# A two-layer diffusion backbone: the first FFN's input half by seven products of quarters, layer 1's adaLN rows beside its output half and the gMLP, the gMLP in a written order

## The chip, the cores and the metric

The kernel runs on one core of a Trainium2 chip. A core has five engines with instruction streams of their own: TensorE (PE: matrix products; PEld is its weight load), VectorE (DVE), ScalarE (ACT), GpSimd (POOL) and SyncE (SP), whose queue issues all the DMAs here. The metric is the device time of one execution, in microseconds (us); less is better.

## The reference, cut to what matters

Two layers over 512 tokens of width 1024. Each layer modulates its input by six rows (shift, scale and gate, for the mixer and for the FFN) made from a conditioning vector, mixes tokens (layer 0: windowed attention; layer 1: a gated MLP over chunks, the gMLP), and then runs a SwiGLU FFN of hidden size 2816.

```
mod_l = silu_c @ ada_w[i] + ada_b[i]
sh_ml, sc_ml, g_ml, sh_fl, sc_fl, g_fl = [m[:, None, :] for m in jnp.split(mod_l, 6, axis=-1)]
h_l = modulate(rmsnorm(x, norm_g[i, 0]), sh_ml, sc_ml)
...                                     # the token mixer gives y_l
x = x + g_ml * rmsnorm(y_l, norm_g[i, 1])
f_l = swiglu(modulate(rmsnorm(x, norm_g[i, 2]), sh_fl, sc_fl), ffn_w_in[i], ffn_w_out[i])
x = x + g_fl * rmsnorm(f_l, norm_g[i, 3])

def swiglu(h, w_in, w_out):
    gate, up = jnp.split(h @ w_in, 2, axis=-1)
    return (jax.nn.silu(gate) * up) @ w_out
```

## The kernel before

All products keep float32 precision by splitting each operand into a high part rounded to the matmul's type (`high`, L197, on ScalarE) and the rest (`low`, L200, mostly on VectorE), and adding three matmuls: high x high, high x low, low x high.

Tokens are four tiles of 128 (t). Weights stream in units of 128 x 2048 (1 MB) through `ws` (two raw buffers, tag raw; four buffers each for the high and low halves). An FFN's input half has 22 units, one for each block of 128 hidden columns (gate and up). Units 0 and 1 are done token tile by token tile (`head`: tiles fa, fat) while the tokens of the turn before still come in. Units 2 to 21 are done by `rest`. The output half is `down`: 11 units, each two blocks of 128 rows; for each unit and token tile 12 matmuls of 512 columns into tile y. Its last two units form the turn: as each token tile's y is done, a `Chain` squares it (ScalarE), makes the root (GpSimd), applies the gate row and adds the residual (`gain_y`, `add_x`, VectorE), squares again, multiplies by the scale row (`gain_x`, GpSimd, L1126), adds the shift row (`shift_x`, VectorE, L1130), and TensorE transposes the result (`turn`, tile hT, L1137), which is split into H, the next stage's input. In the turn out of the attention, tiles 2 and 3 first `merge` a part that was made earlier (L1098).

Layer 0's `rest` makes 8 x 3 matmuls of 512 columns for gate and as many for up: 48 a unit (L1328 to L1330). Layer 1's FFN uses `seven`: the product of the 2 x 2 quarters of H with the 2 x 2 quarters of the unit's weights by seven products with sums and differences of quarters (Strassen's scheme in Winograd's form). Each product is 4 x 3 matmuls of 256 columns, 84 a unit (L1456). The sums of H are made once (`prepare`, inside the turn before: `rebuild` L1375 adds H's parts back on GpSimd, `sum_a` adds on VectorE, and the sums are split); the four differences of each unit's weights by GpSimd (`diff`, L1420); three chains of products collect in PSUM and are combined by `keep`, `up1`, `up2` (L1467), `gate1`, `silu` and `gates`.

The adaLN rows of `Ada(layer, s)`: eight chunks of weights are scaled and added up on VectorE (`add`, L340, tile acc from ada_raw), the sum is split, summed over partitions by two matmuls a half with ones (`total`, L364, tile ada_ps), and `done` (L370 to L374) makes the row. Rows (0, 5) and (1, 0) to (1, 3) are made as a background generator in layer 0's `rest`, four steps a unit; (1, 4) in `down` and the gMLP; (1, 5) in layer 1's `seven`. Their transfers share the tag raw with the weights.

What sets the order: a step is put at a time by `at`, or by its rank in the list ORDER if it stands there; `run_plan` emits the steps, and inside `tc.manual_schedule()` the engines keep that order. Outside of it a scheduler orders the instructions. Before, the turns and layer 1's input half are in a written order; layer 0's `rest`, the output halves' first units and the gMLP are the scheduler's. Each engine runs its own stream in order; the SP queue too.

Of the kernel before, what the change touches and what calls it, by code (L numbers as in the profile page):

```python
# [14 lines left out]
P = 128  # L15
D = 1024
# [134 lines left out]
c0turned_hi_1 wfetch_12 c0turned_hi_0 c1shift_x_1 whigh_12_0 c0turned_lo_0 wlow_11_1 c1turn_0 c0turned_lo_1 c3merge
c1turn_1 head_0_0 c1turned_hi_1 c1turned_hi_0 c2add_x c3gain_y c1turned_lo_1 c1turned_lo_0 head_0_1 c2square_x
c2gain_x c2rstd_x c3square_y c3rstd_y head_1_0 c2shift_x_0 c2shift_x_1 c3add_x c2turn_0 head_0_2 c2turn_1
c2turned_hi_0 c3gain_x c3square_x c3rstd_x c2turned_hi_1 head_1_1 c2turned_lo_0 c2turned_lo_1 whigh_12_1 head_2_0
c3shift_x_0 c3shift_x_1 head_1_2 c3turn_0 c3turn_1 c3turned_hi_1 c3turned_hi_0 c3turned_lo_0 wlow_12_0 c3turned_lo_1
head_2_1 wlow_12_1 head_3_0 head_2_2 head_3_1 head_3_2 work_9_0 wfetch_44 work_10_0 whigh_43_0 whigh_43_1
c0square_y#2 work_9_1 wlow_43_1 work_10_1 work_9_2 wlow_43_0 whigh_44_0 c0rstd_y#2 c0gain_y#2 c0add_x#2 c0gain_x#2
c0square_x#2 c0rstd_x#2 c0shift_x_0#2 c0turn_0#2 work_10_2 whigh_44_1 c1square_y#2 c0shift_x_1#2 wfetch_45
c1rstd_y#2 c1gain_y#2 c1add_x#2 c0turn_1#2 <lambda>_1_2 c1square_x#2 <lambda>_2_2 wlow_44_1 c2square_y#2 c1gain_x#2
whigh_45_0 c1rstd_x#2 work_9_3 c2rstd_y#2 c2gain_y#2 c1shift_x_1#2 c1shift_x_0#2 work_10_3 c2add_x#2 c1turn_0#2  # L160
c0turned_hi_0#2 c0turned_hi_1#2 c2gain_x#2 c0turned_lo_0#2 c1turn_1#2 c3square_y#2 <lambda>_3_2 c1turned_hi_0#2
c1turned_hi_1#2 <lambda>_0_2 c0turned_lo_1#2 c1turned_lo_0#2 <lambda>_0_0 c2square_x#2 c1turned_lo_1#2 c2rstd_x#2
c2shift_x_0#2 <lambda>_1_0 c2shift_x_1#2 wlow_44_0 c3rstd_y#2 c2turn_0#2 c2turn_1#2 c2turned_hi_1#2 c2turned_hi_0#2
c3gain_y#2 c3add_x#2 <lambda>_0_1 c3square_x#2 c2turned_lo_0#2 c3gain_x#2 c3rstd_x#2 <lambda>_2_0 c3shift_x_0#2
c3shift_x_1#2 c2turned_lo_1#2 <lambda>_1_1 c3turn_0#2 whigh_45_1 c3turn_1#2 wlow_45_1 c3turned_hi_0#2
c3turned_hi_1#2 <lambda>_2_1 c3turned_lo_0#2 <lambda>_3_0 c3turned_lo_1#2 wlow_45_0 <lambda>_3_1 wfetch_56
whigh_55_0 work_2_0#2 wlow_55_0 work_3_0#2 whigh_55_1 c0square_y#3 wlow_55_1 whigh_56_0 c0rstd_y#3 c0gain_y#3
# [12 lines left out]
""".split()  # L180


@with_exitstack
def backbone_kernel(ctx: ExitStack, tc: tile.TileContext, a, out):
    nc = tc.nc

    def pool(name, **kw):
        return tc.tile_pool(name=name, bufs=1, reuse_waits="tile", **kw)

    base = ctx.enter_context(pool("base"))  # L190

# [185 lines left out]
    def ada(layer, sections, bank):  # L377
# [18 lines left out]
        for _ in range(4):  # L396
            yield
# [1402 lines left out]
```

## Time and profile before

| | us |
|---|---|
| median of 3 runs (lowest 1154.72, highest 1157.93) | 1154.83 |
| the profiled execution, its own time | 1155.57 |
| its span, first to last instruction | 1153.8 |
| busy: PE 1135.3, DVE 771.0, ACT 507.6, POOL 359.3 | |

The profile is of one execution. Its busy times are sums over each engine's instructions; times in rows are us from the span's start unless marked ns. `x1030` counts instructions, and `<-` names what released a wait. A matmul's own duration overlaps its neighbours', so its cost is read from the spacing of starts. The granted TensorE clock is 0.999 of full speed over the span.

### The profile page before, as it was taken

What the parts mean: (1) busy time and instruction counts of PE and PEld (TensorE: products, weight loads), DVE (VectorE), ACT (ScalarE), POOL (GpSimd) and SP (SyncE); (2) the same over time, 40 slices, a digit from 0 to 9 for tenths busy, and PEclk for the clock granted to TensorE, in tenths of its full rate; (3) what the DMA queues carried; (4) which work ended last, traced back from release to release, by engine and by line L of the source; (5) the groups of instructions that cost most, each with busy time, mean ns of one, the idle gap of its engine ahead of it and who ended that gap; (6) DMA issues with size and microseconds to landing.
All of it is one profiled execution on the core that took longest, in us unless ns stands there. A gap on an engine that the chain in (4) does not pass through costs nothing.

```text
span 1153.8 us, 16530 instructions
## 1 busy us (share of the span) xinstructions
PE 1135.3 (98%) x6638; PEld 974.6 (84%) x6638; DVE 771.0 (67%) x1030; ACT 507.6 (44%) x853; POOL 359.3 (31%) x265
## 2 busy tenths in 40 slices
PE   8999999999999999999999999999999999999997
PEld 5789887778988888888888788889999999998886
DVE  6778989857555566653445758448989998953325
ACT  6357778654313221242233535335454555443322
POOL 2357475514100000000000413007778788700000
PEclk9999999999999999999999999999999999999999
DMA  9633222242155576642435241322133343324221
GB/s 367 273 135 128 78 107 74 97 157 93 74 207 172 204 255 219 223 146 106 167 125 182 87 169 73 110 74 73 56 139 138 126 147 128 129 73 145 74 73 74
DMA packets 25297, 158.10 MB, mean 137 GB/s; under 512 B 3322, under 2 KB 3578, under 8 KB 8452
## 3 DMA queue, kind: packets, MB, share of 16 engines
q1 hardware_dynamic: 25220, 157.04, 38.1%
q8 instruction: 52, 0.85, 0.3%
q14 instruction: 25, 0.20, 0.1%
HBM read 154.94 MB, written 2.10 MB: 136 GB/s over the span
## 4 chain that ended last, share of the span: by engine, by line
PE 84%; DVE 7%; POOL 2%; DMA 2%; issue 2%; ACT 2%; SPq 0%; DVEq 0%; POOLq 0%; ACTq 0%
PE y L252 25%; PE f L1456 13%; PE f L1328 6%; PE f L1330 6%; PE f L1329 6%; PE v L252 3%; PE o_ps L929 2%; PE pT_ps L909 2%; PE s_ps L875 1%; PE u L1690 1%; PE u L1692 1%; PE u L1691 1%; DVE w_lo L200 1%; POOL T L1420 1%; PE s_ps L876 1%
## 5 line engine op out<-in xcount | busy, mean ns | idle before, releaser
L200 DVE TENSOR_TENSOR w_lo<-w_raw,w_hi 128x1024 fp32r<-128x1024 f32 x129 | 171.4, 1336 | 182.9 <-ACT w_hi L197 181.4
L197 ACT CAST w_hi<-w_raw 128x1024 fp32r<-128x1024 f32 x142 | 147.8, 1051 | 308.6 <-PE y L252 140.1
L252 PE MATMUL y<-w_hi,st 128*128 128x512 f32 x928 | 251.1, 390 | 0.0
L252 PEld LDWEIGHTS y<-w_hi,st 128*128 128x128 f32 x928 | 173.6, 188 | 36.0 <-DVE st L200 0.3
L252 PE MATMUL y<-w_lo,st 128*128 128x512 f32 x464 | 144.1, 389 | 0.0
L340 DVE SCALAR_TENSOR_TENSOR acc<-ada_raw,sc,acc 128x1024 f32<-128x1024 f32 x72 | 94.2, 1308 | 61.0 <-DMA ada_raw<-in_ada 60.0
L1328 PE MATMUL f<-H,w_hi 128*128 128x512 f32 x320 | 124.8, 390 | 0.0
L1330 PE MATMUL f<-H,w_lo 128*128 128x512 f32 x320 | 124.6, 389 | 0.0
L1329 PE MATMUL f<-H,w_hi 128*128 128x512 f32 x320 | 124.5, 389 | 0.0
L225 POOL TENSOR_TENSOR ry<-ry,mhalf 128x1 f32<-128x1 f32 x16 | 9.2, 577 | 368.1 <-DVE ry L222 228.6
L252 PEld LDWEIGHTS y<-w_lo,st 128*128 128x128 f32 x464 | 87.1, 188 | 18.3
L1456 PE MATMUL f<-H,w_hi 128*128 128x256 f32 x480 | 89.4, 284 | 1.2 <-DVE fc L1467 1.2
L1420 POOL TENSOR_TENSOR T<-w_raw 128x512 f32<-128x512 f32 x40 | 75.6, 1911 | 36.2 <-DMA w_raw<-in_w 27.0
L1456 PEld LDWEIGHTS f<-H,w_hi 128*128 128x128 f32 x480 | 74.9, 192 | 1.9 <-DVE fc L1467 1.6
L200 DVE TENSOR_TENSOR w_lo<-T,w_hi 128x1024 fp32r<-128x1024 f32 x40 | 72.4, 1809 | 3.4 <-ACT w_hi L197 3.3
L331 POOL MEMSET acc<- 128x1024 f32 x10 | 9.5, 956 | 200.9 <-DVE acc_st L200 200.8
L1330 PEld LDWEIGHTS f<-H,w_lo 128*128 128x128 f32 x320 | 60.1, 188 | 12.6
L1329 PEld LDWEIGHTS f<-H,w_hi 128*128 128x128 f32 x320 | 60.1, 188 | 12.5
L1328 PEld LDWEIGHTS f<-H,w_hi 128*128 128x128 f32 x320 | 60.1, 188 | 12.4
L903 POOL TENSOR_SCALAR p<-p,st 128x512 f32<-128x512 f32 (+1 forms) x64 | 55.9, 889 | 43.6 <-DVE st L899 21.6
L1456 PE MATMUL f<-H,w_lo 128*128 128x256 f32 x240 | 68.0, 283 | 1.0 <-DVE w_lo L200 1.0
L1456 PE MATMUL f<-S,w_hi 128*128 128x256 f32 x320 | 59.3, 283 | 0.0
(246 smaller groups left out, 2514.0 us busy)
## 6 DMA issues: line engine op xcount, KB each, us to landing
w_raw<-in_w SPq DMA_DIRECT2D x87, 1024.0 KB, 4.9
ada_raw<-in_ada SPq DMA_DIRECT2D x36, 1024.0 KB, 4.9
ada<-in_ada SPq DMA_DIRECT2D x8, 1024.0 KB, 10.1
ada_k<-in_ada SPq DMA_DIRECT2D x8, 512.0 KB, 5.7
row<-in_norm_g SPq DMA_DIRECT2D x7, 512.0 KB, 6.7
xin<-in_x SPq DMA_DIRECT2D x4, 512.0 KB, 5.4
x<-in_x SPq DMA_DIRECT2D x4, 512.0 KB, 3.7
out<-x SPq DMA_DIRECT2D x3, 512.0 KB, 2.6
```

What stands on the lines that cost most here:

```text
L197: nc.scalar.copy(out=hi, in_=src)
L200: (eng or nc.vector).tensor_tensor(out=lo, in0=src, in1=hi.bitcast(F32), op=ALU.subtract)
L252: nc.tensor.matmul(dst, l, w[:, n * 512:(n + 1) * 512], start=first and i == 0, stop=last and i == 2)
L340: nc.vector.scalar_tensor_tensor(out=ac, in0=w, scalar=sc[:, k:k + 1], in1=ac, op0=ALU.mult, op1=ALU.add)
L903: nc.gpsimd.tensor_scalar(out=p, in0=p, scalar1=self.st[:, 12 + j:13 + j], scalar2=1.0, op0=ALU.mult, op1=ALU.mult)
L909: nc.tensor.transpose(ps[:, j * P:(j + 1) * P], self.probs[j][:, i * P:(i + 1) * P], ident)
L929: nc.tensor.matmul(self.o[z * HD:(z + 1) * HD, c], v, pt[:, c], start=i < 2, stop=i >= self.nb - 2, tile_position=(0, z * HD), skip_group_ ...
L1328: nc.tensor.matmul(dst, hi, H[:, k, :], start=k == 0, stop=False)
L1329: nc.tensor.matmul(dst, hi, H[:, KC + k, :], start=False, stop=False)
L1330: nc.tensor.matmul(dst, lo, H[:, k, :], start=False, stop=k == KC - 1)
L1420: nc.gpsimd.tensor_tensor(out=T[i], in0=x, in1=y, op=op)
L1456: nc.tensor.matmul(dst, l[:, w], r[:, k, :], start=first and k == 0 and j == 0, stop=k == 3 and j == 2, skip_group_check=True)
```

## The change

1. Layer 0's FFN uses the seven products too: `rest` is now what `seven` was, for both layers, and `first=f0.prepare` puts the sums of its H into the turn out of the attention. Layer 0 keeps the PSUM tiles of two banks (`slot`); its chains 0 and 1 use the two banks of one tile. The written order goes on from that turn to the first steps of the output half.
2. The first half of the sums' sources (`first_half` in place of `rebuild`) is copied from PSUM by ScalarE, in both layers.
3. Row (0, 5) is made in layer 0's `rest` as (1, 5) in layer 1's, by chunks. Rows (1, 0) to (1, 3) are summed beside layer 0's output half (39 steps over its nine first units) from transfers into the two buffers of tag big; (1, 0) and (1, 1) are split whole (`spread`) and finished inside the turn into the gMLP (`rows_b`); (1, 2), (1, 3) and all of (1, 4) in the gMLP.
4. The gMLP's steps, before in program order under the scheduler, are put at times by `at`; ORDER has new ranks for the three turns and for the gMLP (none of its lines is shown).

```diff
-        def rebuild(self, q, t):
+        def first_half(self, q, c):
             name = ("S1", "S4")[q]
-            if t == 0:
+            if c.t == 0:
                 self.sums[name] = self.sum_tile(stage32)
-            dst = self.sums[name][:, :, t * P:(t + 1) * P]
-            hi, lo = (v[:, :, t * P:(t + 1) * P].bitcast(F32) for v in self.A["12" if q else "11"])
-            nc.gpsimd.tensor_tensor(out=dst, in0=hi, in1=lo, op=ALU.add)
+            nc.scalar.copy(out=self.sums[name][:, :, c.t * P:(c.t + 1) * P],
+                           in_=c.pt[:, q * 512:(q + 1) * 512].rearrange("p (k s) -> p k s", k=4))
...
+        def chain(self, n, ch):
+            if ch == 1 and self.bank is slot:
+                return self.pair[n][:, 512:768]
+            self.pair[n] = ps = self.bank(f"f{ch}")
+            return ps[:, 0:256]
...
-        def seven(self):
+        def one_banked(self):
             psM.__exit__(None, None, None)
...
+        def rest(self, nxt_of, head, **kw):
-            T, last, u0 = 10.08, NFF - 1, self.u0
+            T, last, u0, f2 = 10.08, NFF - 1, self.u0, F2[self.layer]
...
-            m5 = Ada(1, 5)
+            m5 = Ada(self.layer, 5)
...
-            run(bg)
+            run(bg, -(-left // (nu - 2 - v)))
+            left -= -(-left // (nu - 2 - v))
...
+    def sums(e, of):
+        e.start(nc.gpsimd)
+        yield
+        for k in range(KC):
+            if k % 2 == 0:
+                e.fetch(k // 2, of)
+            e.add(k)
+            yield
+    def rows_a():
+        for e in m1[:4]:
+            yield from sums(e, big)
+            if e.s < 2:
+                e.fetch_gain()
+                e.spread(f0.p)
+                yield
+    def rows_b(ch):
+        for i, (s, c) in enumerate(((1, 0), (1, 512), (0, 0), (0, 512))):
+            at(7 + .1 * i, m1[s].total, c, slot)
+            at(7.5 + .1 * i, m1[s].done, c)
...
-    f0.rest(to_gmlp, lambda t, n: n < 2 and v_part(t, (n,)), bg)
+    f0.rest(to_gmlp, lambda t, n: n < 2 and v_part(t, (n,)), lend=f0.lend, bg=rows_a(), bg_steps=39, also=rows_b)
...
+    U = 21.8
+    for u in range(4):
+        b = U + 10.9 * u + (2.6 if u == 3 else 0)
         for z in range(2):
+            at(b + 5.45 * z, u_part, u, z)
+            at(b + 5.45 * (z + 1) + .2, gelu_u, u, z)
+            at(b + 5 + 2.5 * z, ws.high, GU + u + 1, z)
+            at(b + 6 + 2.5 * z, ws.low, GU + u + 1, z, nc.vector)
+        at(b - 2, ws.fetch, GU + u + 1)
...
+    for i, e in enumerate(m1[2:4]):
+        at(-6, e.fetch_gain)
+        for c in (0, 512):
+            at(6 + 4 * i + c / 256, e.halve, c, nc.vector)
+            at(25 + 2 * i + c / 512, e.total, c, slot)
+            at(25.6 + 2 * i + c / 512, e.done, c)
...
+    with tc.manual_schedule():
+        run_plan()
```

In the rows of the order that follow, each row is one instruction, or several alike; L200 and L340 of before are L220 and L360 in the changed kernel, L252 is L272, L364 and L365 are L390 and L391.

VectorE in the input half of layer 0's FFN, one unit of before (act is the gated block):

```order
L340 SCALAR_TENSOR_TENSOR acc<-ada_raw,sc,acc 128x1024 x2
L200 TENSOR_TENSOR w_lo<-w_raw,w_hi 128x1024
L340 SCALAR_TENSOR_TENSOR acc<-ada_raw,sc,acc 128x1024 x2
L200 TENSOR_TENSOR w_lo<-w_raw,w_hi 128x1024
L1315 TENSOR_TENSOR act<-f,silu 128x512
```

and one unit of the changed kernel (T holds the differences of weight quarters, fc and f the chains):

```order
L220 TENSOR_TENSOR w_lo<-T,w_hi 128x1024
L220 TENSOR_TENSOR x_4082<-w_raw,x_4082 128x512
L1459 TENSOR_TENSOR act<-fc,silu 128x512
L220 TENSOR_TENSOR w_lo<-T,w_hi 128x1024
L1451 TENSOR_TENSOR f_4122<-f_4122,fc 128x256
L220 TENSOR_TENSOR w_lo<-w_raw,w_hi 128x1024
L1447 TENSOR_TENSOR fc<-f_4050,fc 128x256
L1443 TENSOR_TENSOR fc<-f_4050,fc 128x256
L368 SCALAR_TENSOR_TENSOR acc<-ada_k,sc,acc 128x1024
```

The sums over ada_raw have left the unit; four splits, the combining of the chains and, in every second unit, one chunk of row (0, 5) have come.

VectorE in the output half of layer 0's FFN, about one unit of before (st is the split of a block of act):

```order
L340 SCALAR_TENSOR_TENSOR acc<-ada_raw,sc,acc 128x1024 x2
L200 TENSOR_TENSOR w_lo<-w_raw,w_hi 128x1024
L200 TENSOR_TENSOR st<-act,st 128x512
L200 TENSOR_TENSOR w_lo<-w_raw,w_hi 128x1024
L200 TENSOR_TENSOR st<-act,st 128x512
```

and at the same place of the changed kernel:

```order
L220 TENSOR_TENSOR st<-act,st 128x512
L360 SCALAR_TENSOR_TENSOR acc<-ada_raw,sc,acc 128x1024 x4
L220 TENSOR_TENSOR w_lo<-w_raw,w_hi 128x1024
L220 TENSOR_TENSOR st<-act,st 128x512
L220 TENSOR_TENSOR acc_st<-acc,acc_st 128x1024
L360 SCALAR_TENSOR_TENSOR acc<-ada_raw,sc,acc 128x1024
L220 TENSOR_TENSOR w_lo<-w_raw,w_hi 128x1024
```

Groups of up to four sums, and a whole split, now stand ahead of the next unit's w_lo and st.

TensorE in the turn from layer 0 into the gMLP, from tile 1's second unit of before (y_4879 is token tile 2's y) to the first transpose:

```order
L252 MATMUL y_4866<-w_hi,st 128x512 x2
L252 MATMUL y_4879<-w_hi,st 128x512 x2
L252 MATMUL y_4879<-w_lo,st 128x512 x2
L252 MATMUL y_4879<-w_hi,st 128x512 x4
L252 MATMUL y_4879<-w_lo,st 128x512 x2
L252 MATMUL y_4879<-w_hi,st 128x512 x2
L1137 MATMUL hT<-ident,tmp 128x128 x4
```

and of the changed kernel (y_5917 is tile 2's y), with the rows that only repeat left out between:

```order
L272 MATMUL y_5904<-w_hi,st 128x512 x2
L390 MATMUL ada_ps<-acc_st,ones 128x512
L391 MATMUL ada_ps<-acc_st,ones 128x512
L272 MATMUL y_5917<-w_hi,st 128x512 x2
```

```order
L272 MATMUL y_5917<-w_hi,st 128x512 x2
L390 MATMUL ada_ps<-acc_st,ones 128x512
L391 MATMUL ada_ps<-acc_st,ones 128x512
L390 MATMUL ada_ps<-acc_st,ones 128x512
L391 MATMUL ada_ps<-acc_st,ones 128x512
L272 MATMUL y_5917<-w_hi,st 128x512 x2
L272 MATMUL y_5917<-w_lo,st 128x512 x2
L272 MATMUL y_5917<-w_hi,st 128x512 x4
L272 MATMUL y_5917<-w_lo,st 128x512 x2
L272 MATMUL y_5917<-w_hi,st 128x512 x2
L1139 MATMUL hT<-ident,tmp 128x128 x8
```

Four pairs of ada_ps matmuls have come between tile 1's first unit and tile 2's second, and tile 0's transposes have moved from the middle of tile 2's matmuls to behind them.

## Rows read from the trace of the kernel before

**Rows 1.** The page, part 1: busy us (share of the span) and instructions, TensorE and others.
```profile
PE 1135.3 (98%) x6638; PEld 974.6 (84%) x6638; DVE 771.0 (67%) x1030; ACT 507.6 (44%) x853; POOL 359.3 (31%) x265
```

**Rows 2.** By stretch: from:to, length, busy us (instructions) of each engine, PEclk, DMA share, GB/s.
```profile
303.70:526.50 222.80, 222.80 (x985) 184.27 (x984) 122.52 (x121) 59.42 (x77) 2.88 (x3) 1.00 0.55 194
526.50:630.00 103.50, 103.50 (x457) 85.50 (x456) 46.35 (x48) 30.83 (x40) 0.00 (x0) 1.00 0.41 142
630.00:750.00 120.00, 119.94 (x590) 100.27 (x589) 76.78 (x98) 54.97 (x78) 27.25 (x20) 1.00 0.32 114
820.50:865.00 44.50, 42.76 (x353) 42.15 (x351) 41.02 (x40) 24.52 (x41) 32.17 (x18) 1.00 0.35 123
865.00:1026.00 161.00, 160.00 (x1324) 159.30 (x1325) 144.29 (x139) 84.08 (x146) 115.63 (x57) 1.00 0.36 127
875.70:906.20 30.50, 30.50 (x256) 30.47 (x256) 27.94 (x26) 15.87 (x28) 24.55 (x13) 1.00 0.35 125
```

**Rows 3.** Waits of TensorE, whole run: us in total, times, longest.
```profile
PE f L1456 <- DVE fc L1467: 1.2, 2, 0.7
...
PE f L1456 <- DVE w_lo L200: 1.0, 1, 1.0
```

**Rows 4.** Tile f on TensorE: ns min/median/max, first and last start us, forms.
```profile
L1328 PE MATMUL f<-H,w_hi x320: 389/389/476, 303.7 to 525.8; 128*128 128x512 f32 x160
...
L1456 PE MATMUL f<-H,x x240: 281/283/364, 820.5 to 1016.8; 128*128 128x256 f32 x120
```

**Rows 5.** The chain that ended last, 1000 to 1036 us: start us, us, what.
```profile
1008.38 10.17 PE f L1456 x84
...
1026.19 7.73 PE y L252 x34
1033.93 1.43 PE f L1456 x12
```

**Rows 6.** Tile ada_ps on TensorE by stretch: length, busy us (instructions).
```profile
303.70:526.50 222.80, 5.78 (x20) 1.00 0.55 194
694.50:750.00 55.50, 1.09 (x4) 1.00 0.27 95
```

**Rows 7.** Groups by line, 526.5 to 630 us: busy, mean ns | idle before, releaser.
```profile
L200 DVE TENSOR_TENSOR w_lo<-w_raw,w_hi 128x1024 fp32r<-128x1024 f32 x19 | 23.2, 1221 | 31.4 <-ACT w_hi L197 31.4
...
L340 DVE SCALAR_TENSOR_TENSOR acc<-ada_raw,sc,acc 128x1024 f32<-128x1024 f32 x8 | 10.3, 1285 | 19.1 <-DMA ada_raw<-in_ada 18.9
```

**Rows 8.** VectorE in order of time, 276 to 280 us: start us, us, instruction.
```profile
277.70 1.21 DVE L1098 TENSOR_TENSOR y_part<-y,y_part 128x1024 f32<-128x1024 f32 x1
```

**Rows 9.** Groups by line, 303.7 to 526.5 us.
```profile
L340 DVE SCALAR_TENSOR_TENSOR acc<-ada_raw,sc,acc 128x1024 f32<-128x1024 f32 x40 | 51.3, 1284 | 40.8 <-DMA ada_raw<-in_ada 40.1
```

**Rows 10.** The page, parts 2 (40 slices) and 6 (KB each, us to landing).
```profile
DMA  9633222242155576642435241322133343324221
GB/s 367 273 135 128 78 107 74 97 157 93 74 207 172 204 255 219 223 146 106 167 125 182 87 169 73 110 74 73 56 139 138 126 147 128 129 73 145 74 73 74
...
ada_raw<-in_ada SPq DMA_DIRECT2D x36, 1024.0 KB, 4.9
ada<-in_ada SPq DMA_DIRECT2D x8, 1024.0 KB, 10.1
```

**Rows 11.** All engines in order of time, 626 to 657 us.
```profile
630.21 1.02 ACT L215 ACTIVATE junk<-y 128x1024 bf16<-128x1024 f32 x1 [3.75 <-PE y L252]
...
634.17 2.40 POOL L1126 TENSOR_TENSOR tmp<-x,row 128x1024 f32<-128x1024 f32 x1 [2.02 <-issue]
...
637.11 1.41 DVE L1130 SCALAR_TENSOR_TENSOR tmp<-tmp,rx,row 128x512 f32<-128x512 f32 x2 [1.65 <-POOL rx L225]
...
638.20 0.60 PE L1137 MATMUL hT<-ident,tmp 128*128 128x128 f32 x4
```

**Rows 12.** Groups by line, whole run.
```profile
L372 DVE SCALAR_TENSOR_TENSOR row<-ada_ps,row 128x512 f32<-128x512 f32 x6 | 3.9, 684 | 0.0
...
L370 ACT COPY row<-ada_ps 128x512 f32<-128x512 f32 x6 | 3.5, 586 | 0.1
```

**Rows 13.** Groups by line, 865 to 1026 us.
```profile
L200 DVE TENSOR_TENSOR w_lo<-w_raw,w_hi 128x1024 fp32r<-128x1024 f32 x16 | 30.1, 1884 | 0.0
```

More of the change, by code (lines that the diff above doesn't have):

```diff
@@ L151 @@
[L151 to L155, printed above, removed]
@@ L1251, in down @@
             at(13, ws.fetch, end + 2)
-            for i in range(6 if also is None else 4):
+            for i in range(6 if first is None else 4):
                 u, h = end + i // 2, i % 2
@@ new lines, in lo, with u_part @@
+        def lo(self):
+            low(vlo[:, self.t, :], vhi[:, self.t, :], self.v)
+    u_ps, uTs, mix, ms_ = {}, {}, {}, {}
+    def u_part(u, z):
+        if z == 0:
+            u_ps[u] = slot("u")
+        parts, dst = ws.unit(GU + u), u_ps[u][:, z * 512:(z + 1) * 512]
+        for k in range(KC):
+            hi, lo = (p[:, (k % 4) * 256 + z * P:(k % 4) * 256 + (z + 1) * P] for p in parts[k // 4])
+            nc.tensor.matmul(dst, hi, H1[0][:, k, :], start=k == 0, stop=False)
+            nc.tensor.matmul(dst, hi, H1[0][:, KC + k, :], start=False, stop=False)
+            nc.tensor.matmul(dst, lo, H1[0][:, k, :], start=False, stop=k == KC - 1)
@@ new lines, in backbone_kernel @@
+    at(-9, ws.fetch, GV + 3)
+    at(-8.5, ws_in)
+    at(-8, bias_in)
+    for i in range(3):
+        at(-7.5 + .1 * i, row_in, i)
+    at(-7, ws.fetch, GU)
+    for h in range(2):
+        at(-6 + 2 * h, ws.high, GV + 3, h)
+        at(-5 + 2 * h, ws.low, GV + 3, h, nc.vector)
+        at(2 + 2 * h, ws.high, GU, h)
+        at(3 + 2 * h, ws.low, GU, h, nc.vector)
+    at(0, ws_high)
+    at(1, ws_low)
+    at(1.9, lend_u0)
+    for t in range(NT):
+        c = VChain(t)
+        for u in (2, 3):
+            at(5.45 * t + 2.72 * (u - 2), v_part, t, (u,))
+        for b, f in ((0, c.add), (1.2, c.gelu), (2.5, c.mean), (2.8, c.var), (4.1, c.rstd), (5, c.norm), (5.8, c.gain),
+                     (7, c.bias), (9.6, c.hi), (10.6, c.lo)):
+            at(5.45 * (t + 1) + b, f)
@@ new lines, in backbone_kernel @@
+    for i, e in enumerate(m1[2:4]):
[4 more added lines that the diff above has]
+            at(25.6 + 2 * i + c / 512, e.done, c)
+    e = m1[4]
+    at(14, e.start, nc.gpsimd)
+    for k in range(KC):
+        if k % 2 == 0:
+            at(15 + 3 * k, e.fetch, k // 2)
+        at(22 + 3 * k, e.add, k)
+    at(34, e.fetch_gain)
+    for c in (0, 512):
+        at(47 + c / 256, e.halve, c, nc.vector)
+        at(58 + c / 512, e.total, c, slot)
+        at(58.6 + c / 512, e.done, c)
@@ L1717, in backbone_kernel @@
     down(GO, 4, lambda k: staged(uTs[k]), lambda: V[1, 2], lambda: (V[1, 4], V[1, 3], H2), f1.head, lend=open_f1,
-         also=f1.prepare)
-    f1.seven()
+         first=f1.prepare)
+    f1.one_banked()
+    f1.rest(lambda: None, None, yslot=lambda t: tuple(f1.bank(f"y{t}{n}") for n in range(2)))
+    f1.psE.__exit__(None, None, None)
+    f1.cm.__exit__(None, None, None)
 def _layout(inputs):
```

369 lines of the change are left out of this document (158 added, 211 removed).

## The prediction

> **What bounds the kernel now.** I read four views, each to answer one question: is a late engine or a full one the limit, and in which stage?
>
> The page's first part says that TensorE is at work for 98% of the span [rows 1]. The table by stretch says where that holds [rows 2]: through the first layer's FFN (303.7 to 526.5 its input half, 526.5 to 630 its output half), and through the turn and the gMLP (630 to 750), TensorE's busy time equals the stretch to within 0.1 us. So nothing there waits; only less TensorE work can shorten it, and anything that makes TensorE wait lengthens it one for one. VectorE in the same stretches is busy 122.5 of 222.8 us and 46.4 of 103.5: it has room to take work. The second layer's input half, which already runs by seven products, reads differently: VectorE 144.3 of 161.0 us and GpSimd 115.6, and in its first 44.5 us TensorE is idle for 1.7. Its waits are few: 1.0 us once for a converted weight, 1.2 us in two waits for VectorE's sum that empties a PSUM chain [rows 3].
>
> **The change part by part.**
>
> *The seven products.* A hidden-column block of the first FFN costs 48 matmuls of 512 columns; by the new way it costs 84 of 256. The row-by-row view of tile f gives the two ends of each half [rows 4], and the chain of waits gives one whole block: 84 matmuls in 10.17 us, 121 ns apart [rows 5]. Stage against stage, with all its waits in it: the old way takes 222.8 us from its first f matmul to the first of the output half [rows 2]. The new way, read in layer 1, takes from 820.5 [rows 4] to 1026.19 where the output half begins, and a last product of 1.43 us behind that [rows 5]: 207.1. So **-15.7 us**. Both hold 4 transposes of the head; the old one holds 20 ada_ps matmuls and the new one 4 [rows 6].
>
> The Trainium skill (TensorE: Matmul & The Clock Gate, "Back-to-back issue gap") gives N/2.4 + 2.5 ns for a lone warm matmul of N columns: 109 ns for 256 and 216 for 512. By that, 960 wide ones against 1680 narrow ones would be -23.8 us. The rows disagree: 121 ns here, and 456 wide ones of the output half in 103.5 us are 227 ns each [rows 2]; 1680 x 121 - 960 x 227 = -14.6 us. The extra 11 or 12 ns come with each matmul, wide or narrow, so cutting the work into more pieces pays for it more often. The measurement decides, and the page's figure is in no term.
>
> *The 16 ada_ps matmuls that leave the stage.* They go to the turn (8) and into the gMLP (8 beside the 4 already there), where TensorE has no idle time to hide them. Each is as wide as a y matmul, 103.5 us over 456 [rows 2], 0.23 us: **+3.7 us**.
>
> *Preparing the products in the first layer's first turn.* Eight sums, four splits of the sums and unit 2's parts go to VectorE, four copies from PSUM to ScalarE, four differences of weight quarters to GpSimd. In layer 1 the same list stands in the same turn, and what it costs TensorE is already in the 207.1. What differs: tiles 2 and 3 first merge a kept part, 1.21 us each [rows 8], on VectorE, the engine that TensorE waited for in layer 1 [rows 3]. Bounds: nothing, if the four copies that leave GpSimd give it back, and +3 if both merges and a wait behind them reach TensorE. I take **+0.5**.
>
> *Rebuilding sums on ScalarE in layer 1.* Four GpSimd sums go, and GpSimd reaches its differences sooner, but the waits of the start were VectorE's [rows 3]. Between -1.9 (all idle of the start goes) and +0.5 (ScalarE late): **-0.5**.
>
> *Layer 1's rows beside the output half.* 32 weighted sums of 1.285 us [rows 7] enter it, 8 leave: VectorE goes from 46.4 to about 77, with two whole splits to 80, of some 113 us (the half and the last block before it, where they begin). So VectorE has room, if its data is there. The sums have two buffers of their own, 16 transfers of 1 MB, with 11 MB of weights. A buffer's cycle is two sums and a landing: 2.57 + 4.9 us [rows 10]; eight cycles are 60 us. The last sum stands in VectorE's order three units before the end, so it may be as late as 97 us after the first fetch (the 10 us of the last block and eight units of 10.9). Spare: 37 us. In the order a unit is at most one group of four sums late (5.1 us), and TensorE has one unit of 10.9 us prepared. From 0 to +8 (a wait of 2 us per fetch, what the 40 sums of the old input half show, 40.1 us over 20 fetches [rows 9], on the 16: 80 + 32 - 103.5). I take **+0.6**, near the lower end, since there weights and sums shared two buffers and here they do not.
>
> *The turn and the gMLP.* Rows 0 and 1 of layer 1 are now finished inside the turn. Before, tile 0's y ended at 630.2 and its transpose came 8.0 us later [rows 11]. In the new order TensorE does 48 y matmuls and 8 ada_ps between the two: 12.7 us. The chain that must be done by then: gain and residual on VectorE to +3.9, where GpSimd's product began before [rows 11]; first half of the scale row 0.68 [rows 12], +4.6; two weight splits of 1.22 [rows 7], +7.0; second half, +7.7; GpSimd's product 2.40, +10.1; the shift row's copies, 0.58 [rows 12] behind ada_ps matmuls that end at +10.0, +10.6; the two shifts, 1.41 [rows 11], +12.0. So 0.7 us is left, and the same chain feeds the next tiles with about 1 us. Turn and gMLP together give VectorE eight sums and a few splits and rows more (some 15 us), where it was busy 76.8 of 120 us [rows 2]; the gMLP's slack is larger than the turn's. From 0 to +5 (a missed wait of 2 us on two of the tiles and one more in the gMLP): **+0.8**.
>
> Sum: -15.7 + 3.7 + 0.5 - 0.5 + 0.6 + 0.8 = **-10.6 us**. The profiled execution took 1155.57 us, its span and 1.77 around it; the change makes it 1145.0. The median before is 0.74 lower than that execution, so I forecast **1144.2 us**.
>
> **The rivals.**
>
> *A: VectorE becomes the bound of the first half.* For it: beside GpSimd's differences a w_lo split takes 1884 ns [rows 13], where GpSimd rests 1221 [rows 7]; the new first half gets 80 such differences, and over three blocks of layer 1, which has them, 27.9 of 30.5 us leave 0.85 a block [rows 2]. If layer 0 costs VectorE 1.45 us more a block (its two PSUM chains share one tile, so a wait can be put where layer 1 has none), TensorE waits 0.6 in each, and 20 blocks are +12: 1156, no change. Against it: the order of VectorE there is layer 1's, row for row, and there TensorE is full over those three blocks. (The Trainium skill, SBUF — State Buffer, "SBUF: two separate sides", speaks for this rival: a VectorE operation with two SBUF inputs and a GpSimd operation that reads SBUF exclude one another, each for its whole instruction. The two lengths of the split agree; that TensorE stays full in layer 1 is the trace's own answer to what it costs.)
>
> *B: the data of the rows sets the pace of the output half.* The price is 8 x (2.57 + landing) - 97. At a landing of 4.9 it is negative, at 10.1 (what 1 MB took in the opening, at 367 GB/s and a DMA share of 0.9 or more [rows 10]) it is +4: 1148. From 10.9 us it eats the whole gain, and at 12.5 it is +24: 1168, slower. Against it: 27 MB in 97 us are 292 GB/s, and the slice of 273 GB/s had a share of 0.6 [rows 10].
>
> *C: the turn misses its 0.7 us* and each tile passes it on: +5 in place of 0.8, 1148.
>
> *D: the start's waits vanish* in both layers, since ScalarE now makes the first sums and GpSimd is free: 1.7 us in each [rows 2], with no loss elsewhere: -15.7 + 3.7 - 3.4 = -15.4, 1139.4.
>
> **How the numbers follow.** Forecast 0.60, with its own range 1141 to 1147.5; C 0.14; D 0.12; A 0.07; B 0.07, of which 0.05 beyond 10.9 us. I call 0.3%, 3.5 us, no change (below 1151.4 is faster, above 1158.3 slower). Faster: the forecast, C, D and B's mild part, less a little for C and the forecast going further wrong: 0.86. Same: A and that remainder: 0.08. Slower: 0.06. All lower bounds together give 1139, the upper ones 1159; the range leaves out A and B's far part: 1139 to 1152.
>
> **What would show it.** Right: 1680 f matmuls in the first FFN about 121 ns apart and 207 us from its first to its last; TensorE's idle time from there to the gMLP's end under 3 us; VectorE at 80 us or so in the output half, with its waits for ada_raw there and none of TensorE's behind them; the transpose of tile 0 about 12.7 us behind its y, without a gap. Wrong: gaps of TensorE before w_lo or st in the output half (B), a block of the first half at more than 10.4 us (A), hT or v waiting in the turn (C).

## The result, and the profile after

The changed kernel takes 1140.18 us (median of 4 runs, 1139.60 to 1143.25) against 1155.17 of the kernel before (4 runs): a ratio of 0.9871, 95% interval 0.9847 to 0.9894. A second set gave 1140.49 and 0.9869 (0.9855 to 0.9884). The forecast was 1144.2 with a range of 1139 to 1152: it is faster, as forecast, inside the range, and by 4 us more than forecast. The profiled execution took 1140.33 us, its span 1138.5: 15.3 less than before.

The busy times of the changed kernel from its page, then the weighted sums beside the output half (495 to 615.3 us):

```profile
PE 1121.0 (98%) x7358; PEld 998.8 (88%) x7358; DVE 879.6 (77%) x1140; ACT 565.4 (50%) x983; POOL 488.3 (43%) x341
L360 DVE SCALAR_TENSOR_TENSOR acc<-ada_raw,sc,acc 128x1024 f32<-128x1024 f32 x32 | 41.1, 1283 | 6.5 <-DMA ada_raw<-in_ada 6.1
```

TensorE is as full as before [rows 1] with 14.3 us less of work. VectorE has filled up in the first input half (183.7 of 205.9 us in the table below, 122.5 of 222.8 before [rows 2]), and the 32 sums beside the output half wait 6.1 us for their data where the 40 of the old input half waited 40.1 [rows 9].

The table by stretch answers to [rows 2]: the turn out of the attention, the first input half, the output half, the turn and the gMLP, then layer 1's input half in two rows (after the stretch: its length, busy us and instructions of PE, PEld, DVE, ACT and POOL, the clock, the DMAs' share and GB/s):

```profile
242.70:302.50 59.80, 59.80 (x376) 54.00 (x374) 49.30 (x65) 34.40 (x54) 29.16 (x20) 1.00 0.20 71
302.50:508.40 205.90, 203.63 (x1678) 202.37 (x1677) 183.70 (x180) 105.58 (x186) 138.79 (x77) 1.00 0.39 144
508.40:615.30 106.90, 106.90 (x479) 88.72 (x478) 79.00 (x78) 34.71 (x47) 0.38 (x1) 1.00 0.65 236
615.30:633.10 17.80, 17.80 (x88) 14.69 (x87) 13.65 (x20) 9.18 (x16) 7.97 (x8) 1.00 0.17 60
633.10:736.60 103.50, 103.04 (x511) 86.92 (x510) 75.54 (x94) 46.41 (x68) 22.04 (x14) 1.00 0.44 158
806.40:851.00 44.60, 43.49 (x363) 43.29 (x362) 39.32 (x41) 23.20 (x39) 29.01 (x17) 1.00 0.37 132
851.00:1011.20 160.20, 160.20 (x1333) 160.04 (x1332) 145.85 (x139) 85.25 (x148) 105.05 (x57) 1.00 0.34 125
```

From 508.4 to 633.1 and from 851.0 to 1011.2 TensorE never idles. Behind 302.5 its longer waits are those in the starts of the input halves (1.9 us in layer 0, 1.1 in layer 1), 0.9 in the turn out of the gMLP (tile fa) and 0.5 in the gMLP (tile v). Here are the changed kernel's waits, its chain of waits at the ends of the stages (start, duration, what), and the same places in the chain of before:

```profile
PE f L1432 <- DVE fc L1443: 2.5, 2, 1.4
PE fa L266 <- DVE H L220: 0.9, 1, 0.9
PE f L1432 <- DVE w_lo L220: 0.5, 1, 0.5
PE v L272 <- DVE H L220: 0.5, 1, 0.5
```

```profile
242.85 27.24 PE y L272 x120
508.41 8.87 PE y L272 x39
517.28 1.43 PE f L1432 x12
736.61 38.08 PE y L272 x168
1011.18 7.28 PE y L272 x32
```

```profile
241.98 29.95 PE y L252 x132
526.69 103.50 PE y L252 x456
749.88 38.20 PE y L252 x168
```

Stage by stage, us, from these rows and the first f matmul (303.7 before [rows 4], 302.5 after); the last boundary of before is in [rows 5]:

| stage | before | after | difference |
|---|---|---|---|
| up to the first y of the attention's turn | 242.0 | 242.9 | +0.9 |
| turn out of the attention | 61.7 | 59.6 | -2.1 |
| input half of layer 0, its last product included | 223.0 | 207.3 | -15.7 |
| output half, turn, gMLP (16 ada_ps matmuls came) | 223.2 | 226.8 | +3.6 |
| gMLP's output to layer 1's output half | 276.3 | 274.6 | -1.7 |
| the rest | 127.6 | 127.3 | -0.3 |

The +0.9 is a dip of the clock, to 0.83 over 10 us of the attention, which the profile of before does not have:

```profile
80.00:90.00 10.00, 8.79 (x56) 8.37 (x55) 7.90 (x19) 7.26 (x15) 6.87 (x7) 0.83 0.29 101
```

The second set's profile has the same dip (0.83). The profiles of ten of the experiments below, whose attention is the same, do not have it (1.00 there), so it is not put down to the change; what makes it was not tried.

### The profile page after: what moved, and what is told of

It reads as the page before. It is cut to its first block, busy times and chain, and to the rows that moved or that the text cites. A ratio compares the mean times of both kernels' runs of the same rounds, so it can differ in the third digit from the quotient of the medians.

```text
span 1138.5 us, 18345 instructions
## 1 busy us (share of the span) xinstructions
PE 1121.0 (98%) x7358; PEld 998.8 (88%) x7358; DVE 879.6 (77%) x1140; ACT 565.4 (50%) x983; POOL 488.3 (43%) x341
## 4 chain that ended last, share of the span: by engine, by line
PE 87%; DVE 6%; DMA 2%; issue 2%; ACT 2%; POOL 0%; SPq 0%; DVEq 0%; POOLq 0%; ACTq 0%
PE f L1432 33%; PE y L272 27%; PE v L272 3%; PE o_ps L931 2%; PE pT_ps L911 2%; DMA ada<-in_ada 2%; PE s_ps L877 1%; PE u L1674 1%; PE u L1676 1%; PE u L1675 1%; PE s_ps L878 1%; PE q_ps L264 1%; PE q_ps L266 1%; PE q_ps L265 1%; DVE w_lo L220 1%
## 5 line engine op out<-in xcount | busy, mean ns | idle before, releaser
L272 PE MATMUL y<-w_hi,st 128*128 128x512 f32 x928 | 251.4, 389 | 0.0
L220 DVE TENSOR_TENSOR w_lo<-w_raw,w_hi 128x1024 fp32r<-128x1024 f32 (+1 forms) x109 | 151.5, 1391 | 100.6 <-ACT w_hi L217 100.6
L272 PEld LDWEIGHTS y<-w_hi,st 128*128 128x128 f32 x928 | 173.8, 188 | 36.1
L1389 POOL TENSOR_TENSOR T<-w_raw 128x512 f32<-128x512 f32 x80 | 139.1, 1759 | 111.2 <-DMA w_raw<-in_w 79.3
L1432 PE MATMUL f<-H,w_hi 128*128 128x256 f32 x960 | 178.2, 283 | 2.5 <-DVE fc L1443 2.5
L220 DVE TENSOR_TENSOR w_lo<-T,w_hi 128x1024 fp32r<-128x1024 f32 x80 | 143.4, 1793 | 4.4 <-ACT w_hi L217 4.4
L272 PE MATMUL y<-w_lo,st 128*128 128x512 f32 x464 | 144.2, 389 | 0.0
L1432 PE MATMUL f<-H,w_lo 128*128 128x256 f32 x480 | 135.7, 283 | 0.0
L217 ACT CAST w_hi<-T 128x1024 fp32r<-128x1024 f32 x80 | 83.6, 1046 | 55.0 <-PE f L1432 29.7
L1439 ACT COPY fc<-f 128x256 f32<-128x256 f32 x120 | 44.8, 373 | 122.5 <-PE f L1432 120.0
L272 PEld LDWEIGHTS y<-w_lo,st 128*128 128x128 f32 x464 | 87.0, 188 | 18.0
L1432 PEld LDWEIGHTS f<-S,w_hi 128*128 128x128 f32 x640 | 99.5, 192 | 0.9 <-ACT fc L1439 0.5
L360 DVE SCALAR_TENSOR_TENSOR acc<-ada_raw,sc,acc 128x1024 f32<-128x1024 f32 x64 | 84.9, 1326 | 10.8 <-DMA ada_raw<-in_ada 8.1
L1432 PE MATMUL f<-S,w_lo 128*128 128x256 f32 x320 | 90.7, 284 | 0.5 <-DVE w_lo L220 0.5
L1389 POOL TENSOR_TENSOR T<-w_raw,T 128x512 f32<-128x512 f32 x40 | 82.8, 2070 | 3.1
L1389 POOL TENSOR_TENSOR T<-T,w_raw 128x512 f32<-128x512 f32 x40 | 69.0, 1726 | 3.1
```

The lines of the kernel that those rows point to most:

```text
L217: nc.scalar.copy(out=hi, in_=src)
L220: (eng or nc.vector).tensor_tensor(out=lo, in0=src, in1=hi.bitcast(F32), op=ALU.subtract)
L272: nc.tensor.matmul(dst, l, w[:, n * 512:(n + 1) * 512], start=first and i == 0, stop=last and i == 2)
L360: nc.vector.scalar_tensor_tensor(out=ac, in0=w, scalar=sc[:, k:k + 1], in1=ac, op0=ALU.mult, op1=ALU.add)
L1389: nc.gpsimd.tensor_tensor(out=T[i], in0=x, in1=y, op=op)
L1432: nc.tensor.matmul(dst, l[:, w], r[:, k, :], start=first and k == 0 and j == 0, stop=k == 3 and j == 2, skip_group_check=True)
```

## The experiments

All are changes to the changed kernel; "before" ratios are to the kernel before, run beside them. 1140.5 us is the changed kernel's median in its second set:

> The changed kernel itself once more, for a narrower interval and as the neighbour of the three runs that follow: 1140 +- 1 us, 0.987 of the kernel before.

Measured 1140.49 (4 runs, 1139.84 to 1140.67), ratio 0.9869 (0.9855 to 0.9884), as expected.

**The rows moved, without the products.** Layer 0's input half gets back the 48 wide matmuls a block and row (0, 5) among them:

```diff
-    f0.rest(to_gmlp, ...
+    f0.wide(row_5(), to_gmlp, ...      # the loop of the kernel before
```

> The change without its first part: layer 0's input half keeps the 48 wide matmuls a block (and the scheduler's order, with row (0,5) as before), while layer 1's rows are made beside the output half, in the turn and in the gMLP, whose order is the written one. Theory: TensorE was full before, so moving rows moves TensorE work and saves none: within 2 us of the kernel before, 1153 to 1157, and the whole gain is that of the seven products. Rival: the written order of the gMLP and the two buffers of their own for the rows bring something by themselves: 1148 to 1152, with the rest (8 to 11 us) due to the products. Second rival: the rows alone cost (the output half or the turn waits now, hidden in the sum): above 1158.

It gave 1167.82 us, but by a fault of mine: row (0, 5)'s totals stood right behind its splits, and TensorE waited 7.7 us for acc_st. Once more without it, and with the order of before in the turn out of the attention:

> The rows alone once more, with the fault of the run before taken out: there row (0,5)'s two totals stood right behind its splits in TensorE's order, 7.7 us of waiting of my own making (and a clock at 0.66 behind it). Here the totals come two blocks later, as in the kernel before, and the turn out of the attention has the order of before. Layer 0's input half keeps the 48 wide matmuls; layer 1's rows stand beside the output half, in the turn and the gMLP's written order. Theory: moving rows moves TensorE work and saves none: 1152 to 1157. Rival: the moves cost by themselves (waits in the output half or the turn): 1158 to 1168, as the run before seemed to say. Second rival: the written gMLP brings 4 us or more even without the products: 1147 to 1151.

Measured 1156.66 (12 runs, 1154.76 to 1161.99), ratio 1.0013 (1.0000 to 1.0026): the moves alone bring nothing. The chain shows the stages:

```profile
242.51 29.95 PE y L268 x132
524.20 106.08 PE y L268 x468
750.88 38.08 PE y L268 x168
```

From 524.20 to 750.88 is 226.7, the changed kernel's own 226.8 and 3.5 above before. From 242.51 to 524.20 is 281.7, against 267.0 in the changed kernel (242.85 to 508.41, and the last product of 1.43): the products, their preparation and that turn's order are worth 14.7 us, nearly all of the 14.8 between the two profiled spans (1153.3 and 1138.5).

**The sums' first halves on GpSimd again.**

```diff
-            nc.scalar.copy(out=self.sums[name][...], in_=c.pt[...])
+            nc.gpsimd.tensor_tensor(out=dst, in0=hi, in1=lo, op=ALU.add)   # H's two parts
```

> The changed kernel, with the first halves of two sums made as before the change: GpSimd adds H's two parts (4 per layer), in place of ScalarE's 4 copies from PSUM. Theory: the changed kernel gained more than the forecast because the waits that I charged were never there, and the copies on ScalarE are neutral; then this is 1140 +- 1.5 us, with TensorE idle for 2 us in the 42 us behind the first f matmul of layer 0 and 1 us in layer 1, as in the changed kernel. Rival (D of the prediction): the copies took the waits away, since GpSimd's four sums of 1.3 to 2.0 us each stand ahead of its first differences of weight quarters; then their return makes it 1142 to 1147, with TensorE waiting for w_lo or for the sums' splits in both starts.

Measured 1148.74 (6 runs, 1145.96 to 1153.13), ratio 0.9949 (0.9932 to 0.9966): 8 us slower than the changed kernel, 5.8 between the two profiled spans (1144.3 and 1138.5). The rival's cause holds, but not its place, and the median lies above its range; in the longer runs the mean clock was lower too (0.996 and 0.997, 0.999 in the shorter). GpSimd in the turn out of the attention, in this run and then in the changed kernel:

```profile
285.78 1.29 POOL L1345 TENSOR_TENSOR a_sum<-H 128x512 f32<-128x512 f32 x1
287.03 2.40 POOL L1128 TENSOR_TENSOR tmp<-x,row 128x1024 f32<-128x1024 f32 x1
289.40 1.27 POOL L1345 TENSOR_TENSOR a_sum<-H 128x512 f32<-128x512 f32 x1
290.63 0.99 POOL L245 TENSOR_TENSOR rx<-rx,mhalf 128x1 f32<-128x1 f32 x1
```

```profile
285.42 2.40 POOL L1128 TENSOR_TENSOR tmp<-x,row 128x1024 f32<-128x1024 f32 x1
287.79 0.99 POOL L245 TENSOR_TENSOR rx<-rx,mhalf 128x1 f32<-128x1 f32 x1
```

The sums stand between the two things that the turn itself needs of GpSimd: its product by the scale row and the root rx come 1.6 and 2.8 us later, though this turn began 0.7 us earlier. The shift waits for them, and TensorE for the shift; its waits in and right behind that turn that the changed kernel does not have:

```profile
PE hT L1139 <- DVE tmp L1132: 2.1, 3, 1.0
PE fat L1318 <- DVE silu_a L1309: 0.7, 1, 0.7
```

By stages, first y to output half: +3.7 us in layer 0, +2.6 in layer 1. In layer 1 the new waits are others (0.9 for act, 0.4 more for H, 0.3 for tmp), and GpSimd's part in them was not followed.

**The gMLP left to the scheduler.**

```diff
-    with tc.manual_schedule():
-        run_plan()
+    run_plan()
```

> The changed kernel with the gMLP's steps issued in the same sequence but outside the written order, so that the scheduler may reorder them, as it did before the change. Theory: the gMLP has slack (VectorE 76 of 103.5 us), so TensorE stays full either way: 1140 +- 2 us, TensorE idle under 2 us from the turn to the first y matmul of the gMLP's output. Rival: the written order is what lets the eight more ada_ps matmuls and the splits in without a wait; left to the scheduler the rows and the splits come late: 1143 to 1150, with waits of v or u matmuls for w_lo or H.

Measured 1152.87 (12 runs, 1143.45 to 1156.24), ratio 0.9970 (0.9950 to 0.9990): 12 us slower, the rival and more. TensorE's waits in the turn and the gMLP of the profiled run (1150.70 us), and its clock (third column from the right) behind the second of them:

```profile
PE v L272 <- DVE w_lent L220: 2.4, 1, 2.4
PE mix L266 <- DVE v_lo L220: 0.8, 1, 0.8
PE v L272 <- DVE H L220: 0.8, 1, 0.8
```

```profile
720.00:732.00 12.00, 12.00 (x59) 11.90 (x59) 7.58 (x12) 0.00 (x0) 0.00 (x0) 0.53 0.25 89
```

The waits are 4.0 us. The rest is the clock: 0.53 over 12 us behind a wait of 0.8 among the 128-column mix matmuls, some 6 us lost. The two fastest of the 12 runs, at a mean clock of 0.998, took 1143.45 and 1144.70, about the waits alone (they were not profiled); at 0.992 to 0.988 they took 1150.7 to 1156.2.

**A late row in the turn.** The shift row's totals go 12 y matmuls later:

```diff
-work_9_2 m0total_0_slot m0total_512_slot ... m0done_0 m0done_512 ... work_10_2
+work_9_2 ... work_10_2 m0total_0_slot m0total_512_slot m0done_0 m0done_512
```

> The changed kernel with the two totals of the shift row, and the copies that make the row, 12 y matmuls later in the turn into the gMLP: behind the second unit of tile 2 in place of ahead of it. In the changed kernel the shifts end at 625.5 us and the transposes of tile 0 start at 625.9: 0.4 us to spare. Theory: the row comes at 626.7, the shifts end at 628.1, TensorE waits 2.2 us once before hT and the later tiles follow it: 1142.3, clock as before. Rival: a wait in the middle of full work costs more than itself, since the clock falls behind it, as it did behind 7.7 us of waiting in the first run of the rows alone and in the run under the scheduler: 1147 to 1152. Second rival: the next work covers it: 1140.

Measured 1143.15 (4 runs, 1142.17 to 1145.42), ratio 0.9890 (0.9874 to 0.9907): +2.7, the theory. In the profiled run, the slowest, the clock fell too, for 3 us; the tables show the wait, and the clock a few us behind it:

```profile
PE hT L1139 <- DVE tmp L1132: 2.3, 1, 2.3
```

```profile
632.00:634.00 2.00, 2.00 (x6) 1.54 (x6) 0.45 (x1) 1.63 (x3) 2.00 (x3) 0.50 0.00 0
```

So the turn has next to no slack: what comes late there is lost one for one, sometimes with a piece of the clock on top.

**The rows' transfers through the weights' buffers.**

```diff
-            yield from sums(e, big)
+            yield from sums(e, raw)
```

> The changed kernel with the row transfers beside layer 0's output half put into the two buffers of the weights (tag raw) in place of the two of tag big. Theory: two buffers for 27 transfers are too few: a weight holds one for its landing and two splits (4.9 + about 4 us), a row transfer for its landing and two sums (4.9 + 2.6): 11 x 8.9 + 16 x 7.5 = 218 us over two buffers are 109 us, against 107 us of the half and 10 of the block before it. So no margin: VectorE waits for ada_raw 20 us or more, and TensorE loses 0 to 10 us waiting for w_lo or st: 1141 to 1150. Rival: order within the queue decides, and as weights are fetched first nothing reaches TensorE: 1140.

Measured 1156.46 (10 runs, 1153.94 to 1160.46), ratio 1.0009 (0.9996 to 1.0023): the whole gain is gone, more than I allowed. The waits of TensorE in the half and the turn, and the stretch where they fall:

```profile
PE y L272 <- ACT w_hi L217: 7.9, 1, 7.9
PE ada_ps L390 <- DVE ry L242: 2.7, 1, 2.7
```

```profile
612.00:627.00 15.00, 7.09 (x22) 4.74 (x21) 10.95 (x11) 3.28 (x5) 0.00 (x0) 0.69 0.76 263
```

10.6 us of waiting at the end of the half and, with the clock at 0.69 over that stretch, 16 in all.

**Each row transfer twice.**

```diff
+            for _ in range(2 if of is big else 1):
                 dma(self.raws[u], a["ada"][...])
```

> The changed kernel with each of the 16 row transfers beside layer 0's output half made twice into the same buffer, the second behind the first, 16 MB more. Theory (rival B's price): a buffer's cycle is two landings of 4.9 and two sums, 2.57: eight of them are 99 us against 97, and all transfers of the half are 43 MB in 107 us, 400 GB/s where the opening moved 370: about 10 us of waiting, 1145 to 1155, first of VectorE for ada_raw, then of TensorE for w_lo. Rival: the queue holds the weights' fetches behind the second transfer's wait, so that TensorE waits for weights instead, and by more: above 1155. Second rival: the margin of 37 us covers it: 1140 to 1142.

Measured 1161.18 (4 runs, 1159.58 to 1163.08), ratio 1.0050 (1.0035 to 1.0065), +20.7: above the theory's range, and TensorE waits neither for w_lo nor, as the rival had it, for weights. The first line is TensorE's wait; then the rows' issues of the half and the turn (count, KB each, median us to landing), here and in the changed kernel:

```profile
PE ada_ps L391 <- DVE ry L242: 15.9, 1, 15.9
```

```profile
ada_raw<-in_ada SPq DMA_DIRECT2D x31, 1024.0 KB, 7.3
ada_raw<-in_ada SPq DMA_DIRECT2D x16, 1024.0 KB, 6.2
```

With 7.3 us a landing the pace is 8 x (2 x 7.3 + 2.57) = 137 us; the sums ran from 501 to 636, 135 us. So the formula comes out once the landing is known; the landing that I put in (4.9, a median over the whole run of before) was too short. TensorE stood still from 618 to 633: VectorE's queue held the turn's steps behind the last sums. In the changed kernel the last sum starts at 584.1, three units before the half's end, where the order puts it; with landings of 6.2 the data alone would need 70 us (8 x 8.77) of the 97, so 27 us of the forecast spare of 37 were there.

**Narrow matmuls in the output half.** Each of 512 columns in two of 256 (the half's values are then not the reference's):

```diff
+            if narrow:
+                for n in range(4):
+                    c = slice(n * 256, (n + 1) * 256)
+                    nc.tensor.matmul(ps[:, c], l, w[:, c], ...)
```

> The changed kernel with each matmul of layer 0's output half (512 columns) cut into two of 256: 480 of them become 960, with the same columns in all. Rows of before: 227 ns for a wide matmul and 121 for one of 256, so a pair costs 15 ns more: 480 x 15 = +7.2 us, 1147.4, and the half's matmuls 121 ns apart. The Trainium skill (TensorE: Matmul & The Clock Gate, 'Back-to-back issue gap') by its N/2.4 + 2.5 ns would make a pair 2.5 ns longer than one wide: +1.2 us, 1141.4. A third way: the cost lies in the change of weights, which two pieces under the same weights share; then under +1 us.

Measured 1147.00 (4 runs, 1146.64 to 1147.44), ratio 0.9922 (0.9908 to 0.9936), +6.5. Chain, here and in the changed kernel:

```profile
516.63 105.24 PE y L273 x877
```

```profile
518.71 97.27 PE y L272 x429
```

120.0 ns for a narrow and 226.7 for a wide matmul: 13.3 more for the pair, times 528 (I had counted 480) is 7.0. The Trainium skill's figure for a lone matmul (TensorE: Matmul & The Clock Gate, "Back-to-back issue gap") would have made it 1.3, by estimate; the measurement decides.

**One product less.**

```diff
+                if self.layer == 0:
+                    order = order[:-1]      # product 7 left out
```

> The changed kernel with the seventh product left out of each of layer 0's 20 blocks (its output is not the reference's): 12 matmuls of 256 less a block, 1.45 us of TensorE, the work of the other engines unchanged. Theory: VectorE is the next bound close by: it is busy 9.2 of 10.2 us a block now, so a block falls to 9.2 to 9.6 us, not to 8.7: 12 to 20 us less, 1120 to 1128, with TensorE waiting for w_lo or fc in every block. Rival: TensorE alone sets the block, VectorE's 9.2 us being stretched by its neighbour and elastic: 8.73 us a block, -29 us, 1111.

Measured 1136.36 (4 runs, 1136.01 to 1139.27), ratio 0.9835 (0.9819 to 0.9851): 4 us, not 12 to 29. The first input half in this kernel (in this profile it begins at 307.0; in the changed kernel's row above, at 302.5), and TensorE's longest group of waits in it:

```profile
307.00:507.00 200.00, 181.19 (x1438) 176.51 (x1437) 190.00 (x178) 104.28 (x183) 146.44 (x75) 0.98 0.40 142
PE f L1432 <- DVE fc L1443: 13.4, 10, 1.4
```

240 matmuls, 29 us of TensorE, leave, and the half, first f matmul to first y, is 5.8 us shorter in this profile (200.0 and 205.8). VectorE is at 95% with the same list of work, 6 us longer, and TensorE waits for it (17 times for fc or w_lo, 17.1 us). So the changed kernel stands close to where TensorE and VectorE meet; the theory had the right engine and too much room. How much of the lost room is VectorE's work, and how much its order, which was written for seven products, is not told apart; the clock's mean of 0.98 is in it too.

**VectorE work added.** 32 operations like the rows' sums in the first input half:

```diff
+                    for i in range(2 if n % 5 < 3 else 1):
+                        at(b + 3 + 4 * i, self.same, i)    # x = 0 * x + x
```

> The changed kernel with 32 more VectorE operations in layer 0's 20 blocks by products (one or two a block; each rewrites a token tile of x with its own values, 128 x 1024, the form of the rows' weighted sums): the VectorE work that layer 1's rows would have brought had they stayed in this half, without their transfers. Theory: 1.29 to 1.9 us each makes 2.1 to 3.0 us a block more on VectorE, 11.3 to 12.2 us where TensorE has 10.1: the half gets 22 to 42 us longer, 1162 to 1182, and the products' gain is lost; so the rows had to leave. Rival: VectorE gives way (shorter operations when pressed, 0.9 us of spare a block): under +8 us, below 1148.

Measured 1172.41 (4 runs, 1170.86 to 1173.03), ratio 1.0140 (1.0123 to 1.0158), +31.9: the first theory.

```profile
301.90:539.10 237.20, 215.37 (x1678) 211.88 (x1677) 228.62 (x210) 105.71 (x185) 149.03 (x77) 0.94 0.35 122
```

The half is 31.4 us longer for 32 operations: TensorE waits about 22 us in it, and the clock is at 0.94. Rows that stayed would by this have cost about twice what the products bring; their transfers are not in this run.

**Three steps of VectorE earlier at the starts.**

```diff
-                at(b + 9, self.up1, n)
-                at(b + T + .3, self.up2, n)
+                at(b + (7.6 if n == 2 else 9), self.up1, n)
+                at(b + (7.7 if n == 2 else T + .3), self.up2, n)
-f0part_low_2_2 f0sum_low_S2 ... f0sum_low_S1 ... f0part_low_2_1
+f0part_low_2_2 f0sum_low_S1 ... f0part_low_2_1 f0sum_low_S2
```

> The changed kernel with three steps of VectorE put earlier at the start of each input half: in the first block by products the chains are emptied (up1, up2) before the next split of unit 3, and the low part of unit 2's second weights is made before that of the sum S2. Theory: TensorE's waits of 1.4 us (layer 0) and 1.1 us (layer 1) for VectorE's sum fc, and of 0.5 us for w_lo, are only a matter of what stands ahead of them in VectorE's queue: 2.5 to 3 us less, 1137 to 1138, and no new wait of f. Rival: VectorE is full there (36 of 42.5 us), so what is moved behind the sums is late instead, and the same microseconds are lost at the second products of unit 3: 1139.5 to 1141.

Measured 1138.51 (4 runs, 1138.11 to 1138.94), ratio 0.9855 (0.9842 to 0.9868): the fastest kernel that leaves nothing out, 2 us below the changed one, though the two intervals overlap; the profiled spans are 1.7 apart, 1.3 of it in layer 1. The wait for fc is gone in both starts. In layer 1 nothing replaces it (273.2 us from the gMLP's output to the output half, 274.5 in the second profile of the changed kernel). In layer 0 three waits of 0.5 us, one of them (w_lo) there before, take nearly all of it back:

```profile
PE f L1432 <- DVE w_lo L220: 0.5, 1, 0.5
PE fat L1318 <- DVE silu_a L1309: 0.5, 1, 0.5
PE f L1432 <- ACT fc L1439: 0.5, 1, 0.5
```

## Why the prediction was right, and where it failed

- **The products, -15.7.** Measured -15.7. The way it was made, one layer's stage read for the other's with all its waits, carried the forecast; the rows alone gave 1.0013, so the other parts together add up to nothing there.
- **The 16 matmuls moved, +3.7.** Measured +3.6 for the three stages together, in which one wait of 0.5 us is new (v for H): the 16 cost what was forecast, or a little less.
- **The first layer's preparation, +0.5, and the sums on ScalarE, -0.5: the step that failed.** Measured -2.1 for the turn and -1.7 for layer 1's stages. I wrote that the waits of the start were VectorE's and that GpSimd's four sums gained little by going. What I did not follow is GpSimd's queue inside the turn, where the sums delay its product and root for the next token tile. Putting them back costs 3.7 and 2.6 us. That is what the copies on ScalarE spare; it is not yet the -2.1, since layer 0's turn had no such sums before. There the queue held something else ahead of the root, two clearings of row sums (acc), and TensorE waited behind it for the shift. The kernel before:

```profile
283.44 1.84 POOL L331 MEMSET acc<- 128x1024 f32 x2
285.24 0.55 POOL L225 TENSOR_TENSOR rx<-rx,mhalf 128x1 f32<-128x1 f32 x1
286.72 1.23 PE L1137 MATMUL hT<-ident,tmp 128*128 128x128 f32 x8 [1.34 <-DVE tmp L1130]
```

  The rows alone, with the order of before in that turn, show the same clearings there and the same wait of 1.3 us; the changed kernel shows neither. These are 1.3 of the 2.1; the rest is in no wait that the views list. In layer 1 TensorE's idle time from the gMLP's output to the output half fell from 2.7 to 2.0 us: the waits of the start from 2.2 [rows 3] to 1.1, a wait of 0.5 for a row's split went, and 0.9 in the turn came. The other 1.0 of the 1.7, and what the new order of that turn has to do with it, stays open. Rival D had a part of the cause and, with 1139.4, the nearer time, but not the place: the waits at the starts that it wanted gone are still there (1.9 and 1.1 us).
- **The rows beside the output half, +0.6.** Measured 0: 106.9 of 106.9 us, VectorE 79.0 (about 77 to 80 forecast). The reason given, two buffers of their own, is shown by the run without them, which loses 16 us.
- **The turn and the gMLP, +0.8.** Measured 0 in the turn, 0.5 in the gMLP, and no clock fell. In the turn tile 0's chain was forecast to be done 12.0 us behind its y, 0.7 before it is needed. This is the end of that chain in the trace: GpSimd's product, the shift row's copies, the shifts, then TensorE's transposes:

```profile
621.35 2.40 POOL L1128 TENSOR_TENSOR tmp<-x,row 128x1024 f32<-128x1024 f32 x1
622.93 1.07 ACT L396 COPY row<-ada_ps 128x512 f32<-128x512 f32 x2 [2.52 <-PE ada_ps L391]
624.12 1.41 DVE L1132 SCALAR_TENSOR_TENSOR tmp<-tmp,rx,row 128x512 f32<-128x512 f32 x2 [1.72 <-ACT row L396]
625.91 1.03 PE L1139 MATMUL hT<-ident,tmp 128*128 128x128 f32 x8
```

  Tile 0's y ends at 613.3; the shifts are done at 625.5, 12.2 behind it, and the transposes start 0.4 later. The bound of +5 for missed waits was too low: it counted the waits alone, and three experiments (the scheduler's gMLP, the shared buffers, each transfer twice) paid 12 to 21 us for 4 to 17 us of waiting.
- **Rival A, VectorE as the bound.** I gave it 0.85 us of room a block, in layer 1's rows. The run without one product shows 0.2 to 0.3 (4.1 us of the medians or 5.8 us of the half, over 20 blocks): it did not come true, but by little. The split of raw weights that [rows 13] has at 1884 ns takes 1681 in layer 0's new half, those of differences 1845, so its sizes were about right. The Trainium skill (SBUF — State Buffer, "SBUF: two separate sides") has VectorE's two-input operations and GpSimd's reads of SBUF shut one another out; these lengths, against 1221 ns where GpSimd rests [rows 7], agree.
- **Rival B, the data of the rows.** The formula gives 137 us in the run with each transfer twice, 135 measured, once the landing was known. At the changed kernel's landings, 6.2 us in the median, it gives 70 of the 97 us, so the rival was rightly called unlikely.
- **The range, and luck.** The lower bounds of the parts add up to -15.7 + 3.7 - 1.9 = -13.9, which is 1140.9, not the 1139 that I wrote; only D reaches that. The 1140.2 measured lies below this sum and below the forecast's own 1141 to 1147.5. That it lies in the stated range is owed to D and to this slip: the size of the products was right for its reason, the rest of the sum was 4 us too dear in four of its five other terms.

## What to carry to other kernels

When TensorE is full, a gain in TensorE work counts only if the work it creates elsewhere finds room: make room first (here by moving 32 sums out of the half, with transfers of their own buffers), then cut. Look for the cost of a moved operation in the queue it leaves as well as in the one it enters, above all where that queue holds a step of the next tile. And expect that a wait of TensorE in the middle of full work can cost more than its length.

## What the runs showed of the hardware

A wait of TensorE can be followed by a fall of its clock. In the gMLP left to the scheduler, behind 0.8 us of waiting among 128-column matmuls, the granted clock was 0.53 for 12 us, its 1.2 GHz level for nearly all of it; behind 2.3 us in the turn (the late row) it was 0.50 for about 3 us in the profiled run. The waits of 1.4 us for fc in the changed kernel left it at 1.00. What decides was not tried. Kernels with such waits spread (the scheduler's: 1143 to 1156 us, the longer runs at the lower mean clock), where the changed kernel stays within about 1 us in seven of its eight runs.
